# Scores of the second query half as four 64x64 tiles over 192 keys, with the first half's transposes in the main products' PSUM banks

## The chip, the core and the metric

The kernel runs on one core of one Trainium2 chip. The metric is the device time of one execution in microseconds; the time of a kernel is the median of several executions. TensorE (PE) multiplies matrices and writes to PSUM, of which this kernel uses eight tiles of 128 partitions by 512 float32 values, called banks here. VectorE (DVE) and ScalarE (ACT) read PSUM and write SBUF; GpSimd (POOL) works on SBUF alone; SyncE (SP) issues most DMAs. The engines run their own instruction streams and wait for each other through semaphores.

## The reference

A two-layer decoder trunk on 256 tokens with 2048 channels, in float32. Layer 0 is a Mamba-2 mixer, layer 1 is sliding-window attention with 32 query heads and 4 key/value heads of 64 channels; each is followed by a LayerNorm of `alpha * x + mixer(x)`. The part that matters here is the attention. With a window of 128, a query attends to the 128 keys that end at itself:

```python
s = jnp.einsum("bcqhrd,bckhd->bchrqk", qb, kk).astype(jnp.float32) * (hd ** -0.5)
valid = (diff >= 0)[None] & (diff < WINDOW)[None] & (kpos >= 0)
s = jnp.where(valid[None, :, None, None], s, -jnp.inf)
m = jnp.maximum(jnp.max(s, axis=-1, keepdims=True), sk)
p = jnp.exp(s - m)
p = p / (jnp.sum(p, axis=-1, keepdims=True) + jnp.exp(sk - m))
o = jnp.einsum("bchrqk,bckhd->bcqhrd", p.astype(vv.dtype), vv)
```

The tokens fall into two halves of 128. Queries of the first half see only keys of that half. Query number q of the second half sees the keys q+1 to 127 of the first half and the keys 0 to q of its own: always exactly 128 of the 256 keys.

## The kernel before, in words

Nearly all of the time is a long stream of products on PE: the projections (`mac`, L248, with 256 columns moving; `x_stat`, L972, and `out_unit`, L319 to L321, with 512 columns). Each factor is split into a rounded part and a rest (`wh`/`wl`, L160 on ACT and L163 on DVE), and a product is three passes. Weights come in units of two halves of 512 KB through SP's DMA queue into six buffers for halves, two units ahead of their use. The results stand in four PSUM banks, the pool `mm` (`mm_tile`); everything else on PE (transposes, scores, value products) uses the other four, the pool `ax` (`ax_tile`). A pool hands out the bank whose last use is the longest ago, and a new use waits until its readers on DVE or ACT are done.

The attention layer runs through `B_ORDER`, a list written by hand: a query projection `q` j for each of the four key/value heads, a gate block `g` j, and output blocks `o` j. Each block calls `tick()` after a unit, and small work that was put off with `later(n, fn)` is issued n ticks on, between units of the main stream. So for each j:

- `attend(j, 0)` issues the scores of the first query half, `attend(j, 1)` those of the second. 8 query heads are in 4 blocks of 2; `par` is the head within a block, and its 64 channels are 64 rows of the array, so the two heads are two row tiles of 64 rows and 128 columns (L1087). For the second half a score matmul has 128 queries as weights and all 256 keys moving; a bank of 512 columns takes two of them, so four `ax` banks are filled. float32 matmuls run as two passes, so 8 matmuls are 16 entries in the profile.
- ACT then copies the 128 columns of the query's own half into `p` (L1101), and DVE overwrites, where the key lies after the query (`mask_a0` is not zero there), with the score against the same key number of the first half (L1102). `p` is thus 128 wide: each query has one key for each column. Then come the maximum (L1108), the exponentials on ACT (L1114), and the division (L1119).
- `turn_p` (L1123), some ticks on, transposes `p` on PE into two `ax` banks (L1127), from which DVE (L1138) and ACT (L1136) copy the first half to SBUF; for the second half DVE writes two masked copies (L1131). `pv` multiplies with the values (L1145), as two column tiles of 128 rows and 64 columns.

For j = 0, 1, 2 the tick at which `turn_p` of the first half is due is also that of `attend(j, 1)`, and `turn_p` stands first. For j = 3 `attend(3, 1)` comes one tick after `attend(3, 0)`, and both `turn_p` share a later tick.

Of the kernel before, what the change touches and what calls it, by code (L numbers as in the profile page):

```python
# [8 lines left out]
F32 = mybir.dt.float32  # L9
# [3 lines left out]
U32 = mybir.dt.uint32  # L13
# [4 lines left out]
P = 128  # L18
# [63 lines left out]
def trunk(ctx: ExitStack, tc: tile.TileContext, A: dict, out: bass.AP, dbg=None):  # L82
    nc = tc.nc
    PSUM = bass.MemoryType.PSUM

    def pool(name, bufs=1, side=None, space=None, stack=ctx):
        kw = {"space": space} if space is not None else {}
        return stack.enter_context(
            tc.tile_pool(name=name, bufs=bufs, side=side, reuse_waits="tile", **kw)
        )  # L90

    cst = pool("cst")
# [7 lines left out]
    def nm(s):  # L100
        uid[0] += 1
        return f"{s}_{uid[0]}"
# [4 lines left out]
    def ax_tile():  # L107
        return ax_ps.tile([P, 512], F32, tag="ax", name=nm("ax"), bufs=4)

    cc = cst.tile([P, 896], F32, tag="cc", name="cc")  # L110
    ident = cc[:, 0:128]
    ones = cc[:, 128:256]
    mask_ssd = cc[:, 256:640]

    tri, anti = cc[:, 256:384], cc[:, 640:768]
    mask_a0 = cc[:, 768:896]
    pc = cst.tile([P, PC_END], F32, tag="pc", name="pc")
    eps_t = cst.tile([P, 1], F32, tag="eps", name="eps_t")
    nc.gpsimd.memset(eps_t[:], EPS)
# [134 lines left out]
    def later(n, fn):  # L254
        pending.append([n, fn])
# [723 lines left out]
    kT = bp.tile([P, 4, S], F32, tag="kT", name="kT")  # L979
# [95 lines left out]
    def attend(j, h):  # L1075


        nk = P * (h + 1)
        q2 = qT[j, h]
        p = bp.tile([P, 8, P], F32, tag=f"p{h}", name=nm("p"), bufs=1)  # L1080
        per = 512 // nk
        for b in range(0, 4, per):
            pss = [ax_tile(), ax_tile()]
            for i in range(per):
                for par in range(2):
                    rows = slice(64 * par, 64 * par + 64)
                    nc.tensor.matmul(  # L1087
                        pss[par][:, i * nk : (i + 1) * nk], q2[rows, b + i, :], kT[rows, j, :nk],
                        start=True, stop=True,
                    )  # L1090
            for par in range(2):
                v = p[:, par * 4 + b : par * 4 + b + per, :]
                if h == 0:
                    nc.vector.tensor_tensor(
                        v, pss[par][:].rearrange("p (a k) -> p a k", a=per),
                        mask_a0.unsqueeze(1).to_broadcast([P, per, P]), ALU.add,
                    )
                    continue
                two = pss[par][:].rearrange("p (a c k) -> p a c k", a=per, c=2)

                nc.scalar.copy(v, two[:, :, 1, :])  # L1101
                nc.vector.copy_predicated(  # L1102
                    v, mask_a0.bitcast(U32).unsqueeze(1).to_broadcast([P, per, P]), two[:, :, 0, :]
                )
        sk = snk[:, j * 8 : j * 8 + 8]
        sm = bp.tile([P, 8, 8], F32, tag="sm", name=nm("sm"), bufs=2)
        mx, ng, rs, es, ri = [sm[:, i, :] for i in range(5)]
        nc.vector.tensor_reduce(mx, p[:], AX.X, ALU.max)  # L1108
        nc.vector.tensor_tensor(mx, mx, sk, ALU.max)
        nc.vector.tensor_scalar(ng, mx, -1.0, None, ALU.mult)  # L1110
        nc.vector.tensor_tensor(es, sk, ng, ALU.add)
        nc.scalar.activation(es, es, AF.Exp)
        for r in range(8):
            nc.scalar.activation(  # L1114
                p[:, r, :], p[:, r, :], AF.Exp, bias=ng[:, r : r + 1], accum_out=rs[:, r : r + 1]
            )
        nc.vector.tensor_tensor(rs, rs, es, ALU.add)
        nc.vector.reciprocal(ri, rs)
        nc.vector.tensor_tensor(p[:], p[:], ri.unsqueeze(2).to_broadcast([P, 8, P]), ALU.mult)  # L1119

        pts = {}

        def turn_p():  # L1123
            for par in range(2):
                pt = ax_tile()
                for a in range(4):
                    nc.tensor.transpose(pt[:, a * P : (a + 1) * P], p[:, par * 4 + a, :], ident)  # L1127
                for kc in range(h + 1):
                    t = bp.tile([P, 512], F32, tag="pt", name=nm("pt"), bufs=NPT)
                    if h:  # L1130
                        nc.vector.tensor_tensor(  # L1131
                            t[:].rearrange("p (a q) -> p a q", a=4), pt[:].rearrange("p (a q) -> p a q", a=4),
                            (anti, tri)[kc].unsqueeze(1).to_broadcast([P, 4, P]), ALU.mult,
                        )
                    elif par:
                        nc.scalar.copy(t[:], pt[:])  # L1136
                    else:
                        nc.vector.tensor_copy(t[:], pt[:])  # L1138
                    pts[kc, par] = t

        def pv():
            ov = ax_tile()
            for kc in range(h + 1):
                for par in range(2):
                    nc.tensor.matmul(  # L1145
                        ov[64 * par : 64 * par + 64, :], vt[:, kc, j * 64 : j * 64 + 64], pts[kc, par][:],
                        start=kc == 0, stop=kc == h,
                    )
# [49 lines left out]
    def cols(nb, c0=0, c1=512):  # L1198
        return slice(nb * 512 + c0, nb * 512 + c1)
# [66 lines left out]
    v = xr[:, 1, cols(3, 256)]  # L1266
# [6 lines left out]
def _layout(inputs):  # L1273
# [3 lines left out]
    c = np.ascontiguousarray  # L1277
    a = {}
# [33 lines left out]
    two = lambda v: np.concatenate([v, v])[:, None]  # L1312
# [15 lines left out]
    inv = (np.float64(500000.0) ** (-np.arange(0, 16, 2) / 16.0)).astype(np.float32)  # L1328
    a["inv"] = np.tile(inv[None], (P, 1))
    i = np.arange(P)  # L1330
    cc = np.zeros((P, 896), np.float32)
    cc[:, 0:128] = np.eye(P)
    cc[:, 128:256] = 1.0
    tri = (i[None, :] >= i[:, None]).astype(np.float32)
# [1 line left out]
    cc[:, 384:512] = 1.0  # L1336
    cc[:, 512:640] = tri
    cc[:, 640:768] = 1.0 - tri
    cc[:, 768:896] = np.where(i[None, :] <= i[:, None], 0.0, NEG)
    a["cc"] = cc  # L1340
    return {k: c(v) for k, v in a.items()}
# [20 lines left out]
```

## Time and profile before

| | before |
|---|---|
| time, median of 3 executions | 998.05 us (997.94 to 998.2) |
| span of the profiled execution, first to last instruction | 996.5 us |
| PE busy | 990.9 us, 99% of the span |
| DVE busy | 771.6 us, 77% |
| ACT busy | 567.2 us, 57% |
| score matmuls, L1087 | 1.3% of the span in the chain that ended last |

The profile gives the span of its execution and not that execution's own time; the median lies 1.5 us above this span. "Busy" of PE overlaps from one matmul to the next, so durations of single matmuls don't add up to time; the distance from the start of one group of instructions to the start of the next does. PEld is the loading of weights, which runs ahead of PE. In rows of the timeline the first number is the start, the second the length of the group, and a bracket at the end gives the idle time before it and what ended that.

### The profile page before, as it was taken

What the parts mean: (1) busy time and instruction counts of PE and PEld (TensorE: products, weight loads), DVE (VectorE), ACT (ScalarE), POOL (GpSimd) and SP (SyncE); (2) the same over time, 40 slices, a digit from 0 to 9 for tenths busy, and PEclk for the clock granted to TensorE, in tenths of its full rate; (3) what the DMA queues carried; (4) which work ended last, traced back from release to release, by engine and by line L of the source; (5) the groups of instructions that cost most, each with busy time, mean ns of one, the idle gap of its engine ahead of it and who ended that gap; (6) DMA issues with size and microseconds to landing.
All of it is one profiled execution on the core that took longest, in us unless ns stands there. A gap on an engine that the chain in (4) does not pass through costs nothing.

```text
span 996.5 us, 17887 instructions
## 1 busy us (share of the span) xinstructions
PE 990.9 (99%) x7036; PEld 899.3 (90%) x7036; DVE 771.6 (77%) x1186; ACT 567.2 (57%) x992; POOL 106.4 (11%) x130
## 2 busy tenths in 40 slices
PE   9999999999999999999999999999999999999998
PEld 8999989999999998999999999888988878978976
DVE  7888897867886886786786787898688776676686
ACT  7595856547646645664654764565545544544542
POOL 0001202004003003000300300403000000000003
PEclk9999999999999999999999999999999999999999
DMA  9787587565576666656656456457664546546432
GB/s 364 250 281 300 168 275 213 183 221 178 181 243 184 222 196 192 212 191 210 207 172 227 152 188 219 169 169 244 234 199 144 177 155 192 154 150 200 133 145 84
DMA packets 61555, 198.81 MB, mean 200 GB/s; under 512 B 6848, under 2 KB 11360, under 8 KB 61216
## 3 DMA queue, kind: packets, MB, share of 16 engines
q1 hardware_dynamic: 58528, 188.47, 57.6%
q0 software_dynamic: 2336, 8.69, 2.6%
q8 instruction: 55, 0.90, 0.4%
q10 hardware_dynamic: 608, 0.52, 0.2%
q14 instruction: 28, 0.23, 0.1%
HBM read 195.43 MB, written 2.23 MB: 198 GB/s over the span
## 4 chain that ended last, share of the span: by engine, by line
PE 98%; DVE 1%; issue 0%; ACT 0%; DVEq 0%
PE mm L248 53%; PE mm L972 10%; PE mm L319 9%; PE mm L320 9%; PE mm L321 9%; PE ax L627 2%; PE ax L1087 1%; PE ax L1145 1%; PE ax L603 1%; PE ax L1127 1%; PE ax L586 0%; PE mm L386 0%; PE ax L1050 0%; PE ax L903 0%; DVE wl L163 0%; PE ax L368 0%
## 5 line engine op out<-in xcount | busy, mean ns | idle before, releaser
L163 DVE TENSOR_TENSOR wl<-wr,wh 128x1024 fp32r<-128x1024 f32 (+2 forms) x338 | 392.9, 1182 | 108.7 <-ACT wh L160 106.6
L160 ACT ACTIVATE wh<-wr 128x1024 fp32r<-128x1024 f32 (+2 forms) x338 | 332.6, 1010 | 208.4 <-issue 84.9
L248 PE MATMUL mm<-xH,wh 128*128 128x256 f32 x1280 | 355.7, 278 | 0.0
L248 PE MATMUL mm<-xL,wh 128*128 128x256 f32 x1280 | 354.4, 277 | 0.0
L248 PE MATMUL mm<-xH,wl 128*128 128x256 f32 x1280 | 354.2, 277 | 0.0
L248 PEld LDWEIGHTS mm<-xH,wh 128*128 128x128 f32 x1280 | 241.0, 188 | 1.8 <-ACT wh L194 0.5
L248 PEld LDWEIGHTS mm<-xL,wh 128*128 128x128 f32 x1280 | 241.0, 188 | 1.0
L248 PEld LDWEIGHTS mm<-xH,wl 128*128 128x128 f32 x1280 | 240.8, 188 | 0.0
L319 PE MATMUL mm<-wh,yH 128*128 128x512 f32 x256 | 101.4, 396 | 0.0
L320 PE MATMUL mm<-wh,yL 128*128 128x512 f32 x256 | 99.8, 390 | 0.0
L321 PE MATMUL mm<-wl,yH 128*128 128x512 f32 x256 | 99.7, 389 | 0.0
L643 POOL TENSOR_TENSOR yz<-yz,z 128x256 f32<-128x256 f32 x32 | 32.8, 1033 | 470.4 <-DVE yz L638 470.4
L248 PE MATMUL mm<-x1H,wh 128*128 128x256 f32 x256 | 71.7, 280 | 0.0
L490 DVE SCALAR_TENSOR_TENSOR cv<-mm,pc,cv 128x255 f32<-128x255 f32 x144 | 68.6, 477 | 3.3 <-ACT cv L488 1.9
L248 PE MATMUL mm<-x1L,wh 128*128 128x256 f32 x256 | 70.8, 277 | 0.0
L248 PE MATMUL mm<-x1H,wl 128*128 128x256 f32 x256 | 70.8, 276 | 0.0
L972 PE MATMUL mm<-wh,x1H 128*128 128x512 f32 x160 | 62.9, 393 | 0.0
L972 PE MATMUL mm<-wl,x1H 128*128 128x512 f32 x160 | 61.8, 389 | 0.0
L972 PE MATMUL mm<-wh,x1L 128*128 128x512 f32 x160 | 60.9, 390 | 0.0
L319 PEld LDWEIGHTS mm<-wh,yH 128*128 128x128 f32 x256 | 48.1, 188 | 10.3 <-DVE z L579 1.0
L321 PEld LDWEIGHTS mm<-wl,yH 128*128 128x128 f32 x256 | 48.1, 188 | 10.2
L320 PEld LDWEIGHTS mm<-wh,yL 128*128 128x128 f32 x256 | 48.1, 188 | 9.0
(217 smaller groups left out, 1349.6 us busy)
## 6 DMA issues: line engine op xcount, KB each, us to landing
wr<-in_wa SPq DMA_DIRECT2D x154, 512.0 KB, 5.0
wr<-in_wo SPq DMA_DIRECT2D x64, 512.0 KB, 4.2
wr<-in_wq SPq DMA_DIRECT2D x32, 512.0 KB, 4.5
wr<-in_wg SPq DMA_DIRECT2D x31, 512.0 KB, 4.9
wr<-in_wb SPq DMA_DIRECT2D x16, 512.0 KB, 4.8
wr<-in_wb SPq DMA_DIRECT2D x32, 256.0 KB, 3.6
rb<-rscr SPq DMA_DIRECT2D x11, 512.0 KB, 4.6
wr<-in_wkv SPq DMA_DIRECT2D x8, 512.0 KB, 4.5
```

The costliest lines, as they stand in the source:

```text
L160: m = nc.scalar.activation(h[:, sl], v, AF.Copy)
L163: m = nc.vector.tensor_tensor(l[:, sl], v, h[:, sl].bitcast(F32), ALU.subtract)
L248: m = nc.tensor.matmul(ps, a, b, start=first and i == 0, stop=last and i == 2)
L319: pinned(nc.tensor.matmul(ps, aH[:, k, hs], u.h[:, ks], start=k == 0 and add is None, stop=False), pin)
L320: pinned(nc.tensor.matmul(ps, aL[:, k, hs], u.h[:, ks], start=False, stop=False), pin)
L321: pinned(nc.tensor.matmul(ps, aH[:, k, hs], u.l[:, ks], start=False, stop=k == 3), pin)
L490: nc.vector.scalar_tensor_tensor(a[:, sft:], ps[:, : S - sft], w(3 - sft), a[:, sft:], ALU.mult, ALU.add)
L603: nc.tensor.transpose(ps[:, o : o + P], st.xs[i][:, c * P : (c + 1) * P], ident)
L627: nc.tensor.matmul(ps[64 * r : 64 * r + 64, cols], xd[:, c, r, :], e[:, 256:] if c else e[:, :256], start=c == 0, stop=c == 1,)
L643: nc.gpsimd.tensor_tensor(v, v, st.z[i][:], ALU.mult)
L972: m = nc.tensor.matmul(ps[:], (x1H, x1L, x1H)[i][:, kk, hs], (u.h, u.h, u.l)[i][:, ks], start=(kk, i) == (0, 0), stop=ui == 3 and (k, i) = ...
L1087: nc.tensor.matmul(pss[par][:, i * nk : (i + 1) * nk], q2[rows, b + i, :], kT[rows, j, :nk], start=True, stop=True,)
```

## The change

For the second query half, a score matmul becomes two: 64 queries as weights (a 64x64 tile: 64 channels by 64 queries), and 192 of the 256 keys moving. The first 64 queries of the half see no key above 191, the last 64 none below 64. The two parts of the queries write to the two halves of the partitions of the same bank, the two heads to two banks as before. The queries of the first part stand 64 columns further right, so that for both parts the columns 64 to 191 are what ACT copies, in one instruction as before: for the first part the 128 keys of the first half, for the second part those of its own half. DVE then overwrites a 64x64 block for each part: `copy_predicated` goes from one instruction on 128 partitions and 256 elements to two on 64 partitions and 128 elements each. A new mask (`mask_own`, a lower triangle) joins the constants `cc`, which grow from 896 to 1024 columns.

The first half's `turn_p` takes its two banks from `mm` in place of `ax`.

```diff
-    cc = cst.tile([P, 896], F32, tag="cc", name="cc")
+    cc = cst.tile([P, 1024], F32, tag="cc", name="cc")
+    mask_own = cc[:, 896:960]
...
             for i in range(per):
-                for par in range(2):
-                    rows = slice(64 * par, 64 * par + 64)
-                    nc.tensor.matmul(
-                        pss[par][:, i * nk : (i + 1) * nk], q2[rows, b + i, :], kT[rows, j, :nk],
-                        start=True, stop=True,
-                    )
+                for part in range(h + 1):
+                    for par in range(2):
+                        rows = slice(64 * par, 64 * par + 64)
+                        if h == 0:
...
+                        qs, at = slice(64 * part, 64 * part + 64), i * nk + 64 * (1 - part)
+                        nc.tensor.matmul(
+                            pss[par][qs, at : at + 192], q2[rows, b + i, qs],
+                            kT[rows, j, 64 * part : 64 * part + 192], start=True, stop=True,
+                        )
...
-                two = pss[par][:].rearrange("p (a c k) -> p a c k", a=per, c=2)
-
-                nc.scalar.copy(v, two[:, :, 1, :])
-                nc.vector.copy_predicated(
-                    v, mask_a0.bitcast(U32).unsqueeze(1).to_broadcast([P, per, P]), two[:, :, 0, :]
-                )
+                got = pss[par][:].rearrange("p (a k) -> p a k", a=per)
+
+                nc.scalar.copy(v, got[:, :, 64:192])
+                for part, m, at in ((0, mask_own, 192), (1, mask_a0[:, 64:], 0)):
+                    qs = slice(64 * part, 64 * part + 64)
+                    nc.vector.copy_predicated(
+                        v[qs, :, qs], m[qs].bitcast(U32).unsqueeze(1).to_broadcast([64, per, 64]),
+                        got[qs, :, at : at + 64],
+                    )
...
-                pt = ax_tile()
+                pt = ax_tile() if h else mm_tile()
...
+    cc[:, 896:1024] = np.tril(np.ones((P, P)))
```

In the built program PE's order is otherwise the same: at each of the four places 8 score matmuls become 16, and the transposes of the first half write to `mm` banks. On DVE a few instructions of the main stream (evictions L326 and L330, a split L163) stand one to four places earlier or later; on ACT the last gate's tanh (L1070) stands ahead of the eight exponentials of the last second half (L1114) and not behind them. SP's and POOL's order is unchanged.

More of the change, by code (lines that the diff above doesn't have):

```diff
@@ L1084, in attend @@
             for i in range(per):
-                for par in range(2):
-                    rows = slice(64 * par, 64 * par + 64)
-                    nc.tensor.matmul(
-                        pss[par][:, i * nk : (i + 1) * nk], q2[rows, b + i, :], kT[rows, j, :nk],
-                        start=True, stop=True,
-                    )
+                for part in range(h + 1):
[3 more added lines that the diff above has]
+                            nc.tensor.matmul(
+                                pss[par][:, i * nk : (i + 1) * nk], q2[rows, b + i, :], kT[rows, j, :nk],
+                                start=True, stop=True,
+                            )
+                            continue
+                        qs, at = slice(64 * part, 64 * part + 64), i * nk + 64 * (1 - part)
+                        nc.tensor.matmul(
+                            pss[par][qs, at : at + 192], q2[rows, b + i, qs],
+                            kT[rows, j, 64 * part : 64 * part + 192], start=True, stop=True,
+                        )
             for par in range(2):
@@ L1098, in attend @@
                     continue
-                two = pss[par][:].rearrange("p (a c k) -> p a c k", a=per, c=2)
-                nc.scalar.copy(v, two[:, :, 1, :])
-                nc.vector.copy_predicated(
-                    v, mask_a0.bitcast(U32).unsqueeze(1).to_broadcast([P, per, P]), two[:, :, 0, :]
-                )
+                got = pss[par][:].rearrange("p (a k) -> p a k", a=per)
[5 more added lines that the diff above has]
+                        got[qs, :, at : at + 64],
+                    )
         sk = snk[:, j * 8 : j * 8 + 8]
@@ L1330, in _layout @@
     i = np.arange(P)
-    cc = np.zeros((P, 896), np.float32)
+    cc = np.zeros((P, 1024), np.float32)
     cc[:, 0:128] = np.eye(P)
```

## The prediction

> **What bounds the kernel now.** I read the page's shares and its chain first, then the timeline of PE around the score matmuls, then the waits of PE's weight loads, then DVE's timeline for the banks that change hands.
>
> ```profile
> span 996.5 us, 17887 instructions
> PE 990.9 (99%) x7036; PEld 899.3 (90%) x7036; DVE 771.6 (77%) x1186; ACT 567.2 (57%) x992; POOL 106.4 (11%) x130
> ...
> PEclk9999999999999999999999999999999999999999
> ...
> PE 98%; DVE 1%; issue 0%; ACT 0%; DVEq 0%
> PE mm L248 53%; PE mm L972 10%; PE mm L319 9%; PE mm L320 9%; PE mm L321 9%; PE ax L627 2%; PE ax L1087 1%; PE ax L1145 1%; PE ax L603 1%; PE ax L1127 1%; PE ax L586 0%; PE mm L386 0%; PE ax L1050 0%; PE ax L903 0%; DVE wl L163 0%; PE ax L368 0%
> ```
>
> The chain is PE for 98% of the span, at the full granted clock. So whatever PE saves shows in the time, unless PE then waits for something that it does not wait for now. The score matmuls L1087 are on that chain. One place of the first half and the four of the second, each with the row behind it (the distance of the two starts is what PE spends):
>
> ```profile
> 720.66 1.16 PE L1087 MATMUL ax<-kT,qT 64*128 64x128 f32 x16
> 721.75 0.38 PE L248 MATMUL mm<-x1H,wh 128*128 128x256 f32 x1
> ...
> 738.26 1.04 PE L1127 MATMUL ax<-cc,p 128*128 128x128 f32 x8
> 739.23 2.79 PE L1087 MATMUL ax<-kT,qT 64*128 64x256 f32 x16
> 741.95 0.50 PE L972 MATMUL mm<-wh,x1H 128*128 128x512 f32 x1
> ...
> 791.98 1.03 PE L1127 MATMUL ax<-cc,p 128*128 128x128 f32 x8
> 792.94 2.71 PE L1087 MATMUL ax<-kT,qT 64*128 64x256 f32 x16
> 795.58 0.50 PE L319 MATMUL mm<-wh,oH 128*128 128x512 f32 x1
> ...
> 868.35 2.71 PE L1087 MATMUL ax<-kT,qT 64*128 64x256 f32 x16
> 870.99 0.50 PE L319 MATMUL mm<-wh,oH 128*128 128x512 f32 x1
> ...
> 931.98 2.00 PE L1087 MATMUL ax<-kT,qT 64*128 64x256 f32 x16
> 933.90 0.39 PE L248 MATMUL mm<-x1H,wh 128*128 128x256 f32 x1
> ```
>
> First half (128 keys): 1.09 us. Second half (256 keys): 2.72, 2.64 and 2.64 us for j = 0, 1, 2, and 1.92 us for j = 3; together 9.92 us. The difference between the first three and the last is waiting, as the waits of the weight loads say (total, times, longest):
>
> ```profile
> PEld ax L1087 <- ACT pt L1136: 0.8, 2, 0.4
> ...
> PEld ax L1087 <- DVE pt L1138: 0.5, 1, 0.5
> PEld ax L1087 <- PE ax L1127: 0.5, 3, 0.2
> ...
> PEld ax L1145 <- DVE wl L163: 0.3, 1, 0.3
> ```
>
> In j = 0, 1, 2 two of the four `ax` banks were just filled by `turn_p`, and the third and fourth score bank wait for its copies L1138 and L1136. With the broken pairs of tiles around them these waits cost 2.72 - 1.92 = 0.80 and twice 0.72 us, 2.24 us in all. For j = 3 `turn_p` comes later and there is no such wait.
>
> **The change, part by part.**
>
> *The tiles.* A matmul's own durations say how tiles overlap:
>
> ```profile
> L1087 PE MATMUL ax<-kT,qT x128: 272/374/480, 720.7 to 933.6; 64*128 64x128 f32 x64, 64*128 64x256 f32 x64
> ...
> 758.51 1.08 PE L1145 MATMUL ax<-pt,vt 128*64 128x512 f32 x4
> 759.52 0.33 PE L1127 MATMUL ax<-cc,p 128*128 128x128 f32 x1
> ...
> L1145 PE MATMUL ax<-pt,vt x48: 592/592/643, 758.5 to 959.9; 128*64 128x512 f32 x48
> L386 PE MATMUL mm<-first x32: 272/273/323, 21.5 to 24.3; 128*64 128x128 f32 x32
> L386 PE MATMUL mm<-xr x20: 272/273/273, 22.8 to 23.8; 128*64 128x128 f32 x20
> ```
>
> Row tiles: 16 entries of 256 columns take 1.92 us, 16 of 128 columns 1.09 us. So 128 columns more in each of 8 steps of two tiles cost 0.83 us, 0.104 us a step; a step is 0.104 us for each 128 columns, and 1.92 - 8 x 0.208 = 0.26 us is fixed (the switch of the tiling at both ends and the first weight load). Column tiles overlap as well: four entries of 512 columns, two tiles, take 759.52 - 758.51 = 1.01 us, two steps of 4 x 0.104 us and 0.18 us fixed, where four in a row would take over 1.66 us. No row shows row and column tiles together. If four tiles run at once, 32 entries are again 8 steps, of 192 columns, which lies halfway: (1.92 + 1.09) / 2 = 1.51 us. The first weight load has 64 columns and not 128: it shows as the excess of the first matmul, 480 - 376 ns in L1087 and 643 - 592 ns in L1145, so 0.05 us less: 1.46 us a place, 5.82 us for four before rounding. I take this end of the range, because both ways of overlap that it puts together are seen complete. The other end is one tile at a time, below.
>
> *The waits.* The four score banks are then free long before: the changed program's waits name transposes and scores of earlier ticks. The 2.24 us go; they are within the 9.92 us above. What is late next at this place is only the drain behind the transposes (0.2 us, the third row of the waits), which all places had.
>
> Sum: 9.92 - 5.82 = 4.10 us less on PE.
>
> *The `mm` banks that `turn_p` now takes.* Each must be free of its last reader, and the next main products wait for the other two. The rows for j = 0, j = 1 and j = 3:
>
> ```profile
> 736.15 0.41 DVE L1071 SCALAR_TENSOR_TENSOR sg<-sg,mm 128x256 f32<-128x256 f32 x1
> ...
> 789.32 0.41 DVE L1071 SCALAR_TENSOR_TENSOR sg<-sg,mm 128x256 f32<-128x256 f32 x1
> ...
> 790.78 0.68 DVE L326 SCALAR_TENSOR_TENSOR xr<-xr,mm 128x512 f32<-128x512 f32 x1
> 792.17 0.69 DVE L326 SCALAR_TENSOR_TENSOR xr<-xr,mm 128x512 f32<-128x512 f32 x1 [0.71 <-PE mm L321]
> ...
> 945.88 1.22 DVE L1119 TENSOR_TENSOR p<-p,sm 128x1024 f32<-128x1024 f32 x1
> 947.01 0.68 DVE L330 TENSOR_TENSOR xr<-xr,mm 128x512 f32<-128x512 f32 x1
> ...
> 950.38 1.91 PE L1127 MATMUL ax<-cc,p 128*128 128x128 f32 x16
> ```
>
> By the changed program's banks, `turn_p` for j = 0 needs those of the last two gate products: read by 736.56, needed at 738.26, 1.7 us to spare. For j = 1 read by 789.73, needed at 791.98; 2.2 us, and still 1.0 us if PE comes 1.26 us earlier by j = 0 and DVE doesn't. The main products behind the scores then take the banks of the output products ahead of them: read by 791.46 and 792.86, needed from 795.58 - 2.4 = 793.2 (both gains taken off) and 2.7 us later. For j = 3 read by 947.69 and `p` itself ready by 947.10, for transposes at 950.38 that move with their inputs. Price: nothing; if the cover goes, at most what the old waits cost, 2.24 us. `turn_p`'s own banks are free again when the copies L1138 and L1136 end, within 2 us, and the next product to use them is at least one output unit or a query unit away.
>
> *DVE and ACT.* Eight predicated copies of 64x128 elements in place of four of 128x256 a place:
>
> ```profile
> L1102 DVE COPY_PREDICATED p<-cc,ax x16: 397/439/446, 742.5 to 937.4; 128x256 f32<-128x256 uint32 x16
> ...
> L957 DVE TENSOR_TENSOR rt<-qt,cs x8: 218/222/225, 709.7 to 912.3; 128x64 f32<-128x64 f32 x8
> ...
> 786.00:800.00 14.00, 13.98 (x73) 11.17 (x73) 12.69 (x19) 7.58 (x18) 0.00 (x0) 1.00 0.72 225
> ```
>
> 128 elements a partition lie a third of the way from 64 (222 ns) to 256 (439 ns), 0.29 us: 8 x 0.29 - 4 x 0.44 = +0.6 us on DVE at each place. DVE is 12.69 of 14 us busy around j = 1 (third engine of that row), so it may fall behind by as much there; what waits behind it are the copies for transposes a whole block later and splits `wl` made ahead of use. In the waits only one of 0.3 us on `wl` is left in the attention. I cost this at 0; bounds 0 and 4 x 0.6 us, were all of it to reach PE. ACT's copies keep their 256 elements, and the exponentials of j = 3 that stand later have over 3 us (950.38 - 947.10).
>
> *The constants.* 64 KB more in one DMA on SP, ahead of weight loads.
>
> ```profile
> cc<-in_cc SPq DMA_DIRECT2D x1, 448.0 KB, 8.8
> ...
> 0.00:22.00 22.00, 21.01 (x155) 18.22 (x157) 15.79 (x68) 17.21 (x67) 0.30 (x5) 1.00 0.94 356
> 22.00:60.00 38.00, 38.00 (x359) 37.80 (x354) 32.12 (x58) 23.93 (x41) 1.71 (x4) 1.00 0.77 265
> ```
>
> At 356 GB/s these are 0.18 us of transfers in the busiest stage. PE fills the stage behind it (38.00 of 38.00 us), so the later loads have cover: 0, and 0.18 us without it.
>
> **The sum** is 996.5 - 4.1 = 992.4 us of span. The median stands 1.5 us above this execution's span, so 998.05 - 4.1 = 994.0 us, 0.41% less. About 0.2% (2.0 us) is what a measurement can tell from no change.
>
> **Rivals.**
>
> *Issue binds.* 16 matmuls a place become 32 entries, four in each 0.156 us. The densest stretch of the trace is L386: 52 entries from 21.5 to 24.3, 54 ns each, and there columns (0.104 us for a pair) explain the rate, so it is only a bound. If PE can start no more than one in 54 ns, a place takes 32 x 0.054 + 0.21 = 1.94 us, four 7.75, and the gain is 2.2 us: 995.9. Against it: PE stands behind slow matmuls of 0.23 us just before, time in which instructions can be fetched ahead.
>
> The Trainium skill's page "TensorE: Matmul & The Clock Gate" (section "Wait — 56ns, not 53.3ns?") gives 62 ns a MATMUL of sequencer time where the hardware decoder is off, which binds when the array work is shorter. By it a place would take 32 x 0.062 + 0.21 = 2.19 us and the sum would be 996.9 us, an estimate from that page; L386's 54 ns a matmul is already below it, though over 52 of them only.
>
> *The two parts of the queries take turns* (two by two tiles): 16 steps of 0.156 us, 2.71 us a place, 10.8 in all, so 0.9 us lost in spite of the waits: 999.0, within 0.2%. L1145 and L386, where column tiles overlap, speak against it.
>
> *The tiles run one at a time* in the 64x64 form. 32 x 0.156 + 0.21 = 5.2 us a place, 20.8 us against 9.92: 1009.0, slower. It decides from a step of four tiles above 0.28 us (9.92 / 4 = 2.48 = 8 steps + 0.21), against 0.156 forecast. Against it: every pair of tiles that the trace has overlaps, by rows and by columns. For it: no row has this form.
>
> *The bank wait only moves.* Transposes or main products wait for `mm` banks as long as the scores did for `ax` ones: 2.24 us of the gain gone, 996.2. Against it: the spare times of 1.0 us and more.
>
> The same page (section "Measured speedup vs the span model") puts about 4 ns on each further tile: two more in 32 steps are an estimated 0.26 us, 994.2; no row here resolves it.
>
> **How the numbers follow.** Forecast 0.75, issue 0.07, moved bank wait 0.05, two by two 0.06, one at a time 0.07. The predicted time is the first's, 994.0; its own range is 993.4 (0.6 us of unseen good fortune in DVE's order) to 994.9 (0.9 us of DVE lag reaching PE). The range reaches to the issue rival and the moved wait with the same margin: 993.4 to 996.5, leaving out 0.13 and some tail. Faster by over 0.2%: the first three, 0.87; within: two by two, 0.06; slower: 0.07.
>
> **What would show it.** In the profile after, the score matmuls with 192 columns stand in 32 entries from their first start to the next line in about 1.46 us at all four places, j = 0 like j = 3. No wait of these loads on L1138 or L1136's successors. The transposes of the first half start without a wait on DVE, and the main product behind the scores follows at once. About 2.0 us or more at a place would speak for issue, 2.7 for turns, 5 for one at a time. A main product or transposes that wait on an eviction of an `mm` bank would show the moved wait. The prediction is wrong if the 64x64 form has a cost that neither kind of pair has.

## The result, and the profile after

| | before | after |
|---|---|---|
| time, median | 998.05 us (997.61 to 999.32) | 994.61 us (994.38 to 994.64) |
| span of the profiled execution | 996.5 us | 992.7 us |
| score blocks of the second half, sum of four | 9.92 us | 5.84 us |
| first score matmul to the end of the last output product | 267.63 us | 263.60 us |

The measured ratio is 0.9962, with a 95% interval of 0.9951 to 0.9973: 2.7 to 4.9 us faster, against a forecast of 4.1. The two medians alone lie 3.44 us apart (0.9966). A second series of the same kernel gave 994.37 us and the same ratio.

PE's timeline of the kernel after (start, length, then line and form) at the four places:

```profile
738.61 1.53 PE L1097 MATMUL ax<-kT,qT 64*64 64x192 f32 x32
740.07 0.50 PE L973 MATMUL mm<-wh,x1H 128*128 128x512 f32 x1
...
791.06 1.53 PE L1097 MATMUL ax<-kT,qT 64*64 64x192 f32 x32
792.52 0.50 PE L320 MATMUL mm<-wh,oH 128*128 128x512 f32 x1
...
865.32 1.53 PE L1097 MATMUL ax<-kT,qT 64*64 64x192 f32 x32
866.78 0.50 PE L320 MATMUL mm<-wh,oH 128*128 128x512 f32 x1
...
927.77 1.53 PE L1097 MATMUL ax<-kT,qT 64*64 64x192 f32 x32
929.23 0.39 PE L249 MATMUL mm<-x1H,wh 128*128 128x256 f32 x1
```

From the first start to the next product each block takes 1.46 us: 32 entries, and the same at j = 0, where DVE's copy was late before the change, as at j = 3, where nothing was. The waits of PE's weight loads in the attention (total, times, longest):

```profile
PEld ax L1158 <- issue: 4.3, 14, 0.4
PEld ax L1140 <- ACT wh L161: 2.4, 3, 0.8
...
PEld ax L1097 <- PE mm L1140: 0.5, 3, 0.2
PEld mm L973 <- issue: 0.3, 1, 0.3
```

The rows of the score loads on L1138 and L1136 are gone (those copies are L1151 and L1149 now), and no row names a reader of an `mm` bank. The three waits of up to 0.2 us on PE's own transposes stood there before. The page's shares show the same from afar:

```profile
span 992.7 us, 18034 instructions
PE 986.4 (99%) x7100; PEld 896.6 (90%) x7100; DVE 774.9 (78%) x1202; ACT 566.4 (57%) x992; POOL 105.4 (11%) x130
```

PE has 64 entries more and 4.5 us less to do; DVE 16 instructions and 3.3 us more.

The blocks gave 4.08 us, the profiled span only 3.86. A cut at three points tells where the rest lies. The first point is the first score matmul of j = 0, ahead of everything that the change touches on PE; it stood at 720.66 before:

```profile
720.05 1.16 PE L1090 MATMUL ax<-kT,qT 64*128 64x128 f32 x16
```

The second point is the end of the last output product, before and after:

```profile
988.02 0.28 PE L321 MATMUL mm<-wl,oH 128*128 128x256 f32 x1
```

```profile
983.36 0.28 PE L322 MATMUL mm<-wl,oH 128*128 128x256 f32 x1
```

From the first point to this one, called the stretch below, the time went from 267.63 to 263.60 us: 4.03 less, the blocks' 4.08 but for 0.05. The third point is the end of the span; what lies behind the last product is the tail. At the first point the kernel after was 0.61 us earlier, and the tail was 9.03 us in place of 8.25, 0.78 longer. Neither was in the prediction. The experiments first take the 4.03 apart and then these two.

### The profile page after: what moved, and what is told of

The parts are those of the page before. It is cut to its first block, busy times and chain, and to the rows that moved or that the text cites. A ratio compares the mean times of both kernels' runs of the same rounds, so it can differ in the third digit from the quotient of the medians.

```text
span 992.7 us, 18034 instructions
## 1 busy us (share of the span) xinstructions
PE 986.4 (99%) x7100; PEld 896.6 (90%) x7100; DVE 774.9 (78%) x1202; ACT 566.4 (57%) x992; POOL 105.4 (11%) x130
## 4 chain that ended last, share of the span: by engine, by line
PE 99%; DVE 0%; DVEq 0%; issue 0%
PE mm L249 53%; PE mm L973 11%; PE mm L320 9%; PE mm L322 9%; PE mm L321 9%; PE ax L628 2%; PE ax L1158 1%; PE ax L604 1%; PE ax L1097 1%; PE ax L1090 0%; PE ax L587 0%; PE mm L387 0%; PE ax L1051 0%; PE ax L1140 0%; PE mm L1140 0%; PE ax L904 0%
```

## Experiments

**Each part alone.** `tiles_alone` undoes the bank part, `banks_alone` is the kernel before with the bank part.

```diff
 tiles_alone, against the kernel after
-                pt = ax_tile() if h else mm_tile()
+                pt = ax_tile()
 banks_alone, against the kernel before
-                pt = ax_tile()
+                pt = ax_tile() if h else mm_tile()
```

> Only the tile part of the change: the first half's turn writes to ax banks again. Theory (the two parts overlap, because a score block that issues faster only reaches the occupied banks sooner): the third and fourth score bank come free at the same moment as before the change, about 1.77 us after the block's first load at j=0, 1.69 us at j=1 and 2 and not late at j=3, while the first two banks are now done after about 0.75 us. The waits on the pt copies return and grow to about 1.0, 0.95, 0.95 and 0 to 0.2 us, the blocks last 2.5, 2.4, 2.4 and 1.5 to 1.7 us, 8.8 to 9.0 us together against 9.92, and the gain over the kernel before is about 1.0 us, 997.0. Rival (the parts add up): the waits stay at 0.80, 0.72 and 0.72 us, the blocks sum to 8.1 us and the gain is 1.8 us, 996.2.

> Only the bank part: two tiles of 64x128 over 256 keys as before, with the first half's turn in the main products' banks. Theory: the three waits go and nothing takes their place, so all four blocks last 1.92 us, 7.68 together against 9.92, a gain of 2.24 us, 995.8. Rival (the main bank is late at a place): a new wait stands at the transposes' first load or at the first main product behind the block, and the gain is under 2 us; then the waits named there show it. With tiles_alone: if the parts overlap, the gains of the two alone sum to about 3.2 us, less than the 4.1 us of the blocks with both.

Measured: `tiles_alone` 997.43 us (ratio 0.9993, 0.9984 to 1.0002), `banks_alone` 995.65 us (0.9979, 0.9970 to 0.9988). PE's timeline of `tiles_alone` at j = 0, and two rows of its waits:

```profile
738.54 0.88 PE L1097 MATMUL ax<-kT,qT 64*64 64x192 f32 x16
739.80 1.28 PE L1097 MATMUL ax<-kT,qT 64*64 64x192 f32 x16 [0.38 <-DVE pt L1151]
741.01 0.50 PE L973 MATMUL mm<-wh,x1H 128*128 128x512 f32 x1
```

```profile
PEld ax L1097 <- ACT pt L1149: 1.7, 3, 0.7
...
PEld ax L1097 <- DVE pt L1151: 0.7, 1, 0.7
```

The block of j = 0 breaks in two: the second pair of banks begins 1.26 us after the first (739.80 - 738.54), though the four steps of the first pair take less than 0.75 (half a block of 1.46). The four blocks took 2.47, 2.38, 2.39 and 1.46 us, 8.70 together. That is 1.22 less than before, and the waits are longer than before, as expected: the banks come free no sooner because PE asks sooner. `banks_alone`:

```profile
739.12 2.00 PE L1087 MATMUL ax<-kT,qT 64*128 64x256 f32 x16
741.05 0.50 PE L972 MATMUL mm<-wh,x1H 128*128 128x512 f32 x1
```

All four blocks are 1.93 us, 7.71 together, 2.21 less than before. So the parts alone are worth 1.22 and 2.21 us, 3.43 together, and 4.08 in one kernel: the faster tiles pay in full only where the banks are free. On the median the tile part alone can't be told from no change: its stretch is 1.18 us shorter than before, but its tail is 0.61 longer, for a reason that comes last below.

**What sets the length of a step.** The prediction priced a step by the columns that move. Three kernels change the columns or the number of entries and keep the rest: `four_tiles_256` multiplies each part of 64 queries with all 256 keys (and copies from the bank as before), `eight_tiles` cuts the 128 queries into four parts of 32 (eight 64x32 tiles), `thirds_64` cuts each matmul in three of 64 columns.

```diff
 four_tiles_256 (copies from the bank as in the kernel before)
-   qs, at = slice(64 * part, 64 * part + 64), i * nk + 64 * (1 - part)
+   qs, at = slice(64 * part, 64 * part + 64), i * nk
-   pss[par][qs, at : at + 192], ..., kT[rows, j, 64 * part : 64 * part + 192]
+   pss[par][qs, at : at + 256], ..., kT[rows, j, :256]
 eight_tiles
-                for part in range(h + 1):
+                for part in range(4 * h or 1):
...
-   qs, at = slice(64 * part, 64 * part + 64), i * nk + 64 * (1 - part)
+   hf = part // 2
+   qs, at = slice(32 * part, 32 * part + 32), i * nk + 64 * (1 - hf)
...
-   kT[rows, j, 64 * part : 64 * part + 192], start=True, stop=True,
+   kT[rows, j, 64 * hf : 64 * hf + 192], start=True, stop=True,
 thirds_64
+                for t in range(2 * h + 1):
...
-   pss[par][qs, at : at + 192], ..., kT[rows, j, 64 * part : 64 * part + 192]
+   pss[par][qs, at + 64 * t : at + 64 * t + 64], ..., kT[rows, j, 64 * (part + t) : 64 * (part + t) + 64]
```

> The changed kernel, but each quarter is multiplied with all 256 keys, and the copies from the bank and the mask are those of the kernel before. Theory (the step's length goes by the columns that move, whatever the number of tiles): 8 steps of 0.216 us and a little over 0.15 us around them, 1.88 us a place, 7.5 us together; 1.7 us over the changed kernel, 996.3 to 996.6, and 2.3 us under the kernel before. So cutting the queries brings next to nothing by itself, and all the gain of the tile part comes from the 64 columns that a quarter needn't see. Rival (issue or loads set the pace of 32 entries): the block stays at 1.46 us and the time at 994.6.

> The changed kernel with the queries cut into eighths, eight tiles of 64x32 over the same 192 keys: 64 entries a place in place of 32, the same steps. Theory (a step lasts as long as its columns move, and entries of a step start 7 ns apart): eight tiles run at once, 8 steps of 0.163 us, 1.46 us and at most 0.05 us more a place, no change of the time (994.3 to 994.8). Rival (issue: the 41 ns an entry of the four tiles is already the pace at which TensorE takes them): 64 x 41 ns and 0.15 us, 2.8 us a place, 5.3 us slower, 999.9; the entries of a step would then stand 41 ns apart and not 7. The same time but gaps of 7 ns and steps of four would say that tiles of 32 columns share a place of 64.

> The changed kernel with each of its matmuls cut in three of 64 columns: 96 entries a place, the same columns, tiles and copies. Theory (the step goes by its columns, 0.81 ns a column and 8 ns, with the four tiles at once): 24 steps of 0.060 us and 0.15 us, 1.6 us a place, 0.6 us over the changed kernel in all, 995.1. Rival (the weight load of 64 columns, 0.133 us, has to pass between two entries of a tile): 24 x 0.133 and 0.15, 3.3 us a place, 7.5 us slower, 1002. Rival (issue at 54 to 62 ns a matmul of the queue): 96 entries in 5.2 to 6.0 us a place, 15 to 18 us slower.

PE's timelines at j = 0, in that order:

```profile
738.43 1.96 PE L1097 MATMUL ax<-kT,qT 64*64 64x256 f32 x32
740.32 0.50 PE L973 MATMUL mm<-wh,x1H 128*128 128x512 f32 x1
```

```profile
738.64 1.53 PE L1098 MATMUL ax<-kT,qT 64*32 64x192 f32 x64
740.10 0.50 PE L973 MATMUL mm<-wh,x1H 128*128 128x512 f32 x1
```

```profile
739.27 1.63 PE L1098 MATMUL ax<-kT,qT 64*64 64x64 f32 x96
740.83 0.50 PE L973 MATMUL mm<-wh,x1H 128*128 128x512 f32 x1
```

256 columns: 1.89 us a place, as forecast, and 0.04 less than the 1.93 of two tiles with the same columns. Cutting the queries brings next to nothing; the 64 keys that each part need not see bring the gain. 64 entries in place of 32: 1.46 us, no more. 96 entries of 64 columns: 1.56 us, 16 ns an entry (1.56 / 96). The rival "issue binds" at 54 ns would have made this last block over 5 us; this case shows no such floor. The Trainium skill's page "TensorE: Matmul & The Clock Gate" (section "Wait — 56ns, not 53.3ns?") gives 62 ns a MATMUL where the hardware decoder is off; 16 ns an entry, 32 ns a matmul of two entries, are below that, and no run here tells whether the decoder is on.

The times: `four_tiles_256` 995.85 us (0.9979, 0.9970 to 0.9988), 0.45 us under the 996.3 to 996.6 expected; its stretch of 265.30 us is 1.70 over that of the kernel after, as expected, and its tail is shorter (8.25 us, in the last table). `eight_tiles` took 996.41 us (0.9980, 0.9971 to 0.9989) and `thirds_64` 996.0 us (0.9976, 0.9965 to 0.9986), each above its expectation though the blocks came out. Their stretches from first score to last product are 264.89 and 265.08 us, 1.3 and 1.5 over the kernel after; in `thirds_64` the blocks explain 0.4 of that. The waits of `eight_tiles` between 750 and 800 us have a row that the kernel after lacks:

```profile
PEld ax L1159 <- DVE pt L1145: 1.3, 2, 0.9
```

The value products wait for the masked copies. DVE's timeline of `eight_tiles`, and then of the kernel after, shows why they are late:

```profile
741.90 1.25 DVE L1115 COPY_PREDICATED p<-cc,ax 64x128 f32<-64x128 uint32 x4
744.46 0.69 DVE L1022 TENSOR_TENSOR xr<-xr,gb 128x512 f32<-128x512 f32 x1 [1.31 <-DMA gb<-in_lng]
745.18 1.24 DVE L1115 COPY_PREDICATED p<-cc,ax 64x128 f32<-64x128 uint32 x4
```

```profile
741.87 2.50 DVE L1114 COPY_PREDICATED p<-cc,ax 64x128 f32<-64x128 uint32 x8
744.57 0.69 DVE L1022 TENSOR_TENSOR xr<-xr,gb 128x512 f32<-128x512 f32 x1 [0.20 <-DMA gb<-in_lng]
```

In the program built from `eight_tiles` an instruction that waits for a DMA (L1022, a LayerNorm weight) stands among the eight copies and not behind them, and DVE stood still for 1.31 us with half of them undone. `thirds_64` has the same order (1.23 us idle there) and the same wait on L1145 (1.2 us). So the tiles cost nothing, but the DVE order around j = 0 has little to spare.

**Order of issue.** In the change, part 0 and part 1 alternate, so neighbouring matmuls use different tiles. `part_by_part` exchanges the loops over part and product within two banks; `all_first_parts` issues all eight matmuls of part 0 of a place ahead of all eight of part 1.

```diff
 part_by_part
-            for i in range(per):
-                for part in range(h + 1):
+            for part in range(h + 1):
+                for i in range(per):
 all_first_parts
-        for b in range(0, 4, per):
-            pss = [ax_tile(), ax_tile()]
-            for i in range(per):
-                for part in range(h + 1):
+        banks = [[ax_tile(), ax_tile()] for _ in range(0, 4, per)]
+        for part in range(h + 1):
+            for b in range(0, 4, per):
+                pss = banks[b // per]
+                for i in range(per):
...
+        for b in range(0, 4, per):
+            pss = banks[b // per]
```

> The changed kernel with the loops over part and product exchanged: within a pair of banks both products of the first 64 queries are issued, then both of the second. Same instructions, same tiles, other order. Theory (TensorE starts its entries in program order, and an entry whose tile is busy holds up those behind it): the 8 pairs of products of a place go A, A with B, B with A, A with B, B, five slots of two steps instead of four, so 10 steps of 0.16 us and 0.2 us, 1.84 us a place, 1.5 us over the changed kernel, 996.1. Rival (each tile has a queue of its own, so order doesn't matter): 1.46 us a place and 994.6. Second rival (only two entries ever run at once when a pair of tiles is followed by the same pair, without any overlap at the boundaries): 16 steps, 2.7 us a place, 999.7.

> The changed kernel with all eight matmuls of the first 64 queries of a place issued ahead of all eight of the second 64 (four banks taken at once). With two and two exchanged, the place took 1.51 us and not the 1.84 us of strict program order, so entries do start ahead of earlier ones whose tile is busy. Theory A (each pair of tiles has a queue of its own that takes the whole place): the second parts start some 40 to 100 ns after the first and the place lasts 1.5 to 1.6 us, time as the changed kernel's. Theory B (TensorE looks ahead by a few entries only, at least the two matmuls a tile seen): the second parts start when the first parts' third products do, 2.1 to 2.3 us a place, 2.6 to 3.4 us slower. No overlap at all: 2.75 us a place, 5.2 us slower.

`part_by_part` took 994.32 us (0.9962, 0.9950 to 0.9975), as fast as the change, and `all_first_parts` 998.22 us (1.0004, 0.9994 to 1.0015), all gain gone on the median. The places, in that order:

```profile
738.28 1.58 PE L1097 MATMUL ax<-kT,qT 64*64 64x192 f32 x32
739.79 0.50 PE L973 MATMUL mm<-wh,x1H 128*128 128x512 f32 x1
```

```profile
738.48 2.23 PE L1098 MATMUL ax<-kT,qT 64*64 64x192 f32 x32
740.64 0.50 PE L973 MATMUL mm<-wh,x1H 128*128 128x512 f32 x1
```

1.51 and 2.16 us. (The blocks of `all_first_parts` explain 2.8 us over the kernel after and its stretch is 2.9 us longer; the rest of the 3.6 us by which its median is slower stays open.) Strict program order, my theory for the first run, fell: it asked for 1.84. In the trace of `part_by_part` the first matmul of part 1 starts 27 ns after the first of part 0, though the second products of part 0 stand ahead of it and start only when their tiles are free. (The rows don't name the part; but entries of one tile start at least 0.16 us apart, so the third entry, 27 ns behind the first and 20 behind the second, is on another tile.) But PE does not look ahead without end. In `all_first_parts` part 1 starts 0.71 us after part 0, just when part 0's third product enters its tiles. At that moment only the fourth product (one matmul for each of the two tiles) is passed over, as in `part_by_part` only the second was. Both places fit one rule: a tile can hold one waiting matmul beside the one that runs, and the next stops the queue. They fit as well a rule that counts over all tiles, that a matmul may start ahead of at most two others; no run here parts the two. A step is 0.163 us from start to start in the trace; four steps of part 0 alone and then a place like that of `part_by_part` make 4 x 0.163 + 1.51 = 2.16 us, as measured. The Trainium skill's page "TensorE: Matmul & The Clock Gate" (section "The mechanism") calls matmuls strictly first in, first out; that differs from these two traces, and the traces decide.

**VectorE's cover.** `copies_2x` makes each predicated copy twice.

```diff
-                for part, m, at in ((0, mask_own, 192), (1, mask_a0[:, 64:], 0)):
+                for part, m, at in 2 * ((0, mask_own, 192), (1, mask_a0[:, 64:], 0)):
```

> The changed kernel with every predicated copy made twice (16 a place instead of 8, the second writes the same values): 8 x 0.303 = 2.4 us more of VectorE at each place. Theory (VectorE's work there has cover: normalized scores are ready 5.2, 6.5, 6.5 and 2.8 us ahead of their transposes): no change of the time within 0.3 us and no new wait of TensorE. Rival (VectorE is short of time there and hands its lag on through the splits): up to 2.4 us at a place, 9.7 us in all, 1004, and then the 0.8 us that the change itself adds to VectorE at a place would have cost up to 3 us.

996.05 us (0.9980, 0.9971 to 0.9988), 1.5 us slower than the change, where I expected none. The stretch is 264.98 us, 1.4 more, and all of it is one stall at j = 3, where the second half's transposes wait for `p`. PE's timeline there, and in the kernel after the same rows:

```profile
946.28 1.03 PE L1140 MATMUL mm<-cc,p 128*128 128x128 f32 x8
948.48 1.06 PE L1140 MATMUL ax<-cc,p 128*128 128x128 f32 x8 [1.17 <-ACT wh L161]
```

```profile
945.70 1.03 PE L1140 MATMUL mm<-cc,p 128*128 128x128 f32 x8
946.58 1.04 PE L1140 MATMUL ax<-cc,p 128*128 128x128 f32 x8
```

The row names ACT, but what comes last is DVE's division, which ends at 948.33 in `copies_2x` and at 943.80 in the kernel after:

```profile
947.11 1.22 DVE L1132 TENSOR_TENSOR p<-p,sm 128x1024 f32<-128x1024 f32 x1
```

```profile
942.57 1.23 DVE L1132 TENSOR_TENSOR p<-p,sm 128x1024 f32<-128x1024 f32 x1
```

At j = 3 the cover is 2.8 us (946.58 - 943.80), the shortest of the four; the 2.4 us of copies made `p` nearly 4 us later (4.53 less the 0.57 us by which this profile runs behind), so other work of VectorE came in between. At j = 0, 1, 2 the same 2.4 us cost nothing.

**The constants, the start and the tail.** `cc_small` keeps `cc` at 448 KB and makes the mask on GpSimd. `half_copies` leaves half of the predicated copies out. `turn_copies_dve` moves ScalarE's copy of the first half's second transpose to VectorE. `after_again` is the changed kernel itself.

```diff
 cc_small
-    cc = cst.tile([P, 1024], F32, tag="cc", name="cc")
+    cc = cst.tile([P, 896], F32, tag="cc", name="cc")
...
-    mask_own = cc[:, 896:960]
+    own = cst.tile([P, 64], F32, tag="own", name="own")
+    mask_own = own[:]
...
+            nc.gpsimd.tensor_tensor(own[:], anti[:, :64], ident[:, :64], ALU.add)
 half_copies
-                for part, m, at in ((0, mask_own, 192), (1, mask_a0[:, 64:], 0)):
+                for part, m, at in ((0, mask_own, 192),):
 turn_copies_dve
-                    elif par:
-                        nc.scalar.copy(t[:], pt[:])
                     else:
                         nc.vector.tensor_copy(t[:], pt[:])
```

> The changed kernel once more, for the size of the gain and for its spread. Theory: score blocks of 1.46 us at all places, a stretch from the first score block to the last product of 263.6 us as in its first profile, 4.0 us under the kernel before; the rest of the span (start, last store) moves by some tenths from run to run. Median 994.3 to 994.9. If start and tail are a property of the kernel, the first score block stands at 720.05 and the tail lasts 9.03 us again.

> The changed kernel with the constants' tile of 448 KB as before; the 64x64 mask is made on GpSimd from two constants that are there (one addition, ahead of the first scores). It asks whether the 64 KB cost time and where the difference between 4.08 us of the score blocks and 3.44 us of the medians lies. Theory (the difference is spread of runs, start and last store, not the load): 994.3 to 994.8, the same as the changed kernel, and a first score block at 719.7 to 720.7 us in either. Rival (the load costs what is missing): 0.6 us less than the changed kernel, 994.0. In the profiles so far the kernels with 512 KB reach the first score block 0.5 to 0.9 us earlier than those with 448 KB; if that is the load's place, this one reaches it at 720.5 to 720.7.

> The changed kernel without the predicated copy of the second 64 queries (their older keys stay unmasked values of the other block; part of the mask is left out): 4 predicated copies a place, as many VectorE instructions as before the change. In all seven profiles so far with the split copies, 8 KB of program are loaded 2.4 to 2.9 us ahead of the end, among the last stores, and the tail from the last product is 8.55 to 9.03 us; in the three with 4 copies a place there is no such load and the tail is 8.24 or 8.25. Theory (the longer program moves a block of it into the tail): no load in the tail, tail 8.25 us, and the stretch from the first scores to the last product stays at 263.6; median 0.4 to 0.8 us under the changed kernel, 993.7 to 994.2. Rival (the tail comes from something else in the tiles' part): tail 8.6 to 9.0 us and 994.4 to 994.6.

> The changed kernel with ScalarE's copy of the first half's second transpose (one a place, 128x512) on VectorE, like its first: 4 instructions fewer on ScalarE, 4 of 0.68 us more on VectorE. The trace shows 1216 rows on ScalarE in the three kernels without a program load in the tail, and 1218 or 1219 in those that have one; VectorE's rows don't part them (1534 in the kernel before without it, 1533 in the one with half the copies that has it). Theory (ScalarE's program, longer by two or three waits, crosses the end of an 8 KB block): about 1215 rows, no load in the last 8 us, tail 8.25 us instead of 8.6 to 9.0, the stretch from the first scores to the last product 263.6 us since VectorE's 0.68 us a place have cover; median 0.4 to 0.7 us under the changed kernel, 993.8 to 994.2. Rival (the load is tied to something else of the tiles' part): the load and a tail of 8.6 to 9.0 us stay, 994.4 to 994.6. If VectorE's lag reaches TensorE, a new wait on the copies stands in the stretch, which grows by up to 2.7 us.

In the table, "ScalarE rows" are all rows of this engine in the trace, its waits for semaphores included; a program load is a packet of the queue `instruction` (8 KB) between the last product and the end of the span.

| | median | ratio, interval | first score | stretch | tail | ScalarE rows | program load in the tail |
|---|---|---|---|---|---|---|---|
| before | 998.05 | | 720.66 | 267.63 | 8.25 | 1216 | no |
| banks_alone | 995.65 | 0.9979 | 720.55 | 265.45 | 8.24 | 1216 | no |
| four_tiles_256 | 995.85 | 0.9979 | 719.87 | 265.30 | 8.25 | 1216 | no |
| after | 994.61 | 0.9962 | 720.05 | 263.60 | 9.03 | 1219 | yes |
| after_again | 994.37 | 0.9962, 0.9950 to 0.9974 | 720.40 | 263.59 | 8.63 | 1219 | yes |
| cc_small | 994.67 | 0.9968, 0.9956 to 0.9980 | 720.42 | 263.59 | 9.03 | 1219 | yes |
| half_copies | 994.84 | 0.9971, 0.9960 to 0.9981 | 719.62 | 263.60 | 8.70 | 1218 | yes |
| turn_copies_dve | 994.42 | 0.9960, 0.9946 to 0.9973 | 720.47 | 263.69 | 8.25 | 1215 | no |

The stretch repeats to 0.01 us in the first four kernels of the table that have the whole change, though one of them has half the copies; it is the sharpest measure of the change. The start is spread: the same kernel has 720.05 and 720.40. Over all fourteen profiles the kernels with 448 KB of `cc` stand at 720.42 to 720.66 and those with 512 KB at 719.62 to 720.70, so the larger `cc` does not show as a delay, and its 64 KB cost nothing that can be seen.

The tail is 8.25 us or 8.63 to 9.03, and what parts the two is a program load. The DMA view of the last 8 us of the kernel after (queue, packets; then stores, KB, median us to landing):

```profile
q14 instruction: 1, 0.01, 0.7%
issues: line engine op xcount, KB each, median us to landing
...
out<-xr SPq DMA_DIRECT2D x3, 128.0 KB, 2.7
```

One packet of 8 KB of program moves among the last stores, and they land after 2.7 us. The single packets show how. The last 288 packets of stores on SP's queue begin 6.00 us behind the last product; before the change all of them are done at 6.84. After it 270 are done at 6.85, the load lasts from 6.15 to 7.03, and the other 18, a sixteenth of the 288, follow it from 7.03 to 7.72, as if they stood behind it on one of the 16 DMA engines. Queue 1 of the kernel after from 990.6 to 991.5 us, 7.0 to 7.9 us behind the last product:

```profile
q1 hardware_dynamic: 18, 0.02, 5.2%
```

In `turn_copies_dve` the packet of program is not there:

```profile
out<-xr SPq DMA_DIRECT2D x3, 128.0 KB, 2.0
```

`half_copies` has as many VectorE instructions as the kernel before and still has the load, so my first reason (VectorE's longer program) fell. ScalarE's fits all fourteen profiles: 1215 or 1216 rows without the load, 1218 or 1219 with it. The change gives ScalarE no work, but four more waits ahead of the exponentials (three rows more in all, since elsewhere one wait came and two went). `turn_copies_dve`, made to take four instructions from ScalarE, lost the load and had the tail of 8.25 us. That it also took VectorE's work up is no rival to this, since the kernels with more VectorE work have the load. The medians do not show the 0.4 to 0.7 us that I expected from it: 994.42 against 994.61 and 994.37, within the spread of the start, and the ratios of 0.9960 and twice 0.9962 don't either. So what the load costs is shown by the profiles alone.

## Why the prediction was right

The time was 994.6 where 994.0 was forecast, inside the likeliest case's own range of 993.4 to 994.9.

- *The tiles.* 1.46 us a place forecast, 1.46 measured at all four; 5.84 against 5.82 in sum. The block priced from pairs of row tiles and pairs of column tiles held for four tiles, and at 256 columns too (8 x 0.208 + 0.21 = 1.87 us, 1.89 in `four_tiles_256`). How it was split was a little off: a step is 0.163 us in the trace and not 0.156, with 0.15 around the eight and not 0.21. With eight steps the two make the same sum. With 24 they don't: 24 x 0.052 + 0.21 = 1.46 us, against 1.56 in `thirds_64`, so a step costs some ns beside its columns.
- *The waits on the pt copies.* All gone, 2.21 us in `banks_alone` against 2.24 forecast. The sum of blocks was right because both parts were taken together; a sum of two separate gains would have been wrong by 0.65 us (4.08 - 3.43).
- *The `mm` banks at a price of nothing.* Right: no wait names a reader of an `mm` bank, in `banks_alone` either.
- *VectorE.* The copy took 0.303 us against 0.29 estimated:

```profile
L1114 DVE COPY_PREDICATED p<-cc,ax x32: 244/303/309, 741.9 to 934.4; 64x128 f32<-64x128 uint32 x32
```

  8 x 0.303 - 4 x 0.44 = 0.66 us a place, and its cost of 0 held: `half_copies` takes four copies a place away and the stretch stays at 263.60. That this cover has an end was underrated: `copies_2x` reached it at j = 3.
- *The constants.* 0 held, by `cc_small`.
- *The sum.* This is the step that was off. It took the whole span to shrink by the blocks' gain: 996.5 - 4.1 = 992.4. Measured: -4.08 in the blocks, +0.05 elsewhere in the stretch, -0.61 at the start, +0.78 in the tail, 992.7. The start is spread. The tail is a cost of the change that I left out: I counted its instructions on PE and VectorE and took ScalarE's as unchanged, and did not see that a few more waits move a load of program in among the last stores. That the span came within 0.3 us of the forecast is partly luck, since the start and the tail nearly cancel. The rest of the 0.6 us is the distance from span to median, 1.5 us in the forecast and 1.9 after. The 1.5 set the median beside the span of another execution: in the later series every execution of the kernel before took 1.7 to 2.3 us longer than its own span, so by that the profiled one, of 996.5 us, was an estimated 0.4 us slower than the median. The stretch's 4.03 us less a tail longer by 0.4 to 0.8 are 3.2 to 3.6, where the medians show 3.44.
- *The rivals.* Issue at 54 ns (1.94 us a place), turns two by two (2.71), one tile at a time (5.2) and the moved bank wait are all excluded by the blocks of 1.46 us and the waits. What `all_first_parts` does by its order, 2.16 us a place, lies between the forecast and turns. Entries of a step start 7 ns apart in these traces, and that lies beside the columns: eight tiles took the same 1.46 us as four. The Trainium skill's page "TensorE: Matmul & The Clock Gate" (section "Measured speedup vs the span model") puts about 4 ns on each further tile. Three small readings of the prediction don't hold, and nothing hangs on them: the moved wait at 996.2 would have been 1.85 us faster, short of the 2.0 that it set as tellable; the wait for the drain of the transposes stood at three of the four places; and just ahead of the scores stand transposes 0.12 us apart, at j = 3 products 0.11 apart, not matmuls of 0.23.

What stays open: why the start moves by up to 1 us between profiles, which end of a block in ScalarE's program the load follows, and whether TensorE's look-ahead is counted by tile. No kernel tried was faster than the change by more than the spread.

## What to carry to other kernels

Price a packed matmul by the columns that one tile streams, not by the number of tiles or entries; so look for columns that a part of the queries does not need, and issue the tiles in turn, since TensorE passes over a few waiting matmuls only. A faster block waits longer for its banks: free the banks in the same change, or a part of the gain stays behind (here 0.65 of the 1.87 us between blocks of 7.71 and 5.84 us). When a small change is measured on the whole kernel, cut the trace at instructions that the change does not touch: the stretch repeated to 0.01 us where the medians moved by some tenths.

## What was not expected of the hardware

- A matmul starts ahead of an earlier one whose tile is busy: 27 ns after the first entry in `part_by_part`. It doesn't pass over many: in `all_first_parts` the first matmul of part 1 starts after 0.71 us, when one matmul for each busy tile is left ahead of it.
- Eight 64x32 tiles run at once, starting 7 ns apart, in the time of four: 64 entries in 1.46 us. Entries of 64 columns pass at 16 ns each.
- A load of 8 KB of program among the last stores goes with a tail that is 0.4 to 0.8 us longer (8.63 to 9.03 us against 8.25), and two or three rows of ScalarE's program part the kernels in which it falls there (1218 or 1219 rows) from the others (1215 or 1216).
